# Keeping the recurrence layer in its emitted order on every engine, in a two-layer backbone kernel

## The chip, the cores and the metric

The kernel runs on one core of one Trainium2 chip. The metric is device time in microseconds (us) of one execution, and a comparison is made on medians of several runs on the same chip. The core has a matrix engine (TensorE, PE in the profile; its weight loads are shown apart as PEld), a vector engine (VectorE, DVE), a scalar engine (ScalarE, ACT), a further vector engine (GpSimd, POOL) and a queue that issues DMAs (SyncE, SP). Each engine takes its own instructions strictly in order, and waits on semaphores for what other engines and DMAs have to deliver.

## The reference, cut to what matters

Two layers over a context of 256 tokens and a latent sequence of 256 tokens, width 1024, each a mixer followed by a squared-ReLU MLP. Layer 0 mixes with a diagonal state space layer, layer 1 with a gated DeltaNet, which is the recurrence that the change is about. It has 8 key heads and 16 value heads of 128, chunks of 64 tokens, and both directions:

```python
q, k, v, z, gates = h @ w_in            # projections, a short centred conv on q, k, v, l2 norm of q, k
lower = strict(k_beta @ k.T * decay)    # one 64x64 triangle for each chunk and head
t_mat = triangular_solve(lower + eye, eye)
u, w = t_mat @ (v * beta), t_mat @ (k_beta * exp(g))
for each chunk:                          # the chain: one step after the other
    v_new = u_i - w_i @ state
    out_i = (q_i * exp(g)) @ state + attention(q_i, k_i) @ v_new
    state = state * exp(g_last) + k_end.T @ v_new
y = gated_rmsnorm(out, z) @ w_out
```

## The kernel before, in words

Layer 1's recurrence is `gdn_phase` (2003). It treats the 8 key heads with their two value heads each as 8 pairs p = 0 to 7. The weights stream from HBM: `w_load` (1086) loads one 128x1024 block on SP into one of four buffers `wraw`, and `w_split` (1096) makes it two parts in two buffers each, `whi` on ACT and `wlo` in two halves on POOL or DVE, after which `gdn_proj` (1566) multiplies it on PE, three products for each (`hh,whi`, `hl,whi`, `hh,wlo`). There are 49 such projections, 1200 matmuls: for each pair one of keys and two of values with 512 columns, one of queries and two of the output gate `z` with 256, and one for the decay gates. `post_qk`, `post_v`, `post_z` (1623, 1682, 1697) take them from PSUM: ACT copies to `pp`, DVE runs the five-tap conv as steps on `cacc`, and normed heads are transposed. `gdn_gates` (1463) makes the decays on DVE once at the start.

The triangular solve is `gdn_t` (1708), for each pair and each direction d. It loads decay rows by DMA on SP (tile `X`, from `grd`), makes `X` on POOL, DVE and ACT, `N` on DVE and POOL, `U` on DVE, its transpose `T`, and then squares up on PE with `A`, `T` and `U` going through DVE between the matmuls (`ap`, `up`, `wp`), down to `ub`. `X` and `N` have two buffers. The serial part is `gdn_chain` (1793), one for each value head, both heads of a pair side by side. Each of its eight laps multiplies the state with the keys (`c<-S,kt`), makes the residual `r` on DVE, multiplies by the solve's `ub` (`c<-r,ub`), scales to `v` on ACT, multiplies with the keys (`c<-v,kn`) and updates the state `S` on DVE. Three chains may be open at once. `gdn_read` (1867) makes the outputs and `gdn_out` (1909) the product with `w_out` at the end.

Two orders exist. The kernel's own planner, `drive` (316), runs these tasks as generators on a model of the clock, picks whose step can start first, ties going to the lower priority number, and emits the step's instructions. With `clock.fill` set (2096) the model may place a step in an earlier gap of its engine, so that the emitted order is not the order of its planned times. That stretch ends when all solves of pair 7 and all 49 projections have ended; what is left of the layer is emitted with `fill` off (2099). Behind the planner stands the tile scheduler of the compiler. It is given a priority with each instruction, `base + prio * 20000 + n` (263), where n counts the emitted instructions and `prio` is 0 for chains and weight loads, 1 for solves, 2 for reads, 3 for the steps after projections and the splits, 4 for projections and 5 for w_out. It moves instructions on an engine's queue by it. `follow` (124) ties a few PE instructions to earlier ones. The call by which every engine's instruction is emitted is `Engine.call` (259).

Of the kernel before, what the change touches and what calls it, by code (L numbers as in the profile page):

```python
# [252 lines left out]
class Engine:  # L253
# [3 lines left out]
    def __getattr__(self, op):  # L257
        f = getattr(self.eng, op)
        if not callable(f):
            return f  # L260

        def call(*args, **kw):
            c = self.clock
            p = c.issue(self.name, op, args, kw)
            if c.prio is not None:
                c.tc.cur_priority = c.base + c.prio * 20000 + c.n
                c.n += 1
            r = f(*args, **kw)  # L268
            if c.window is not None and self.name == "tensor" and c.prio is not None:
                c.follow(p[0], r.ins)  # L270
            return r
        return call
# [1944 lines left out]
```

## Time and profile before

| What | us |
|---|---|
| median of three runs | 1634.49 |
| the three runs | 1637.27, 1630.75, 1634.49 |
| the profiled execution | 1630.61 |
| its span in the trace | 1628.8 |
| PE busy in the span | 1467.9 |
| DVE busy | 1105.0 |
| ACT busy | 777.4 |
| POOL busy | 654.3 |

The span runs from the first to the last instruction in the trace, 1.8 us less than the execution's time. Layer 1's recurrence begins at about 752 us with its first projection; its first chain starts at about 898, its last projection ends near 1324, and the product with w_out ends near 1428. Before it lie layer 0 and the vectors of the modulation, behind it the last MLP. Busy shares over the whole span mix these stages, so a stretch is read with the busy time of that stretch.

### The profile page before, as it was taken

The page shows a single profiled execution, that of the slowest core. Times are in us where ns is not written, and L with a number is a line of the kernel's source. Part 1 is how long each engine was busy: PE and PEld are TensorE (multiplying, and loading weights), DVE is VectorE, ACT ScalarE, POOL GpSimd, SP SyncE. Part 2 cuts the span into 40 slices and gives each one's busy share as a digit, 9 for nine tenths or more (in the row PEclk, how much of TensorE's full clock was granted, in tenths as well). Part 3 has the DMA queues.
Part 4 walks back from the last instruction along what each step waited for, and adds up shares of the span by engine and source line. Part 5 has one row for each costly group of instructions (what it writes and reads, how often), then busy time and mean ns, then how long its engine had stood idle before and what let it go on. Part 6 is the DMA issues. An engine that isn't in the chain of part 4 may idle for free.

```text
span 1628.8 us, 31232 instructions
## 1 busy us (share of the span) xinstructions
PE 1467.9 (90%) x12370; PEld 1115.7 (68%) x12370; DVE 1105.0 (68%) x2011; ACT 777.4 (48%) x1637; POOL 654.3 (40%) x510
## 2 busy tenths in 40 slices
PE   6895678989999999997968898989999999989998
PEld 2454456767777777786756676767766665689997
DVE  6977798763343343347998878687869765667666
ACT  3352646543222232216456655656565755554443
POOL 3977033622333233334766543343615400014432
PEclk7997889999999999998989999999998999989999
DMA  9786623463544545331222211111211111536552
GB/s 279 264 290 91 137 98 118 156 211 113 172 147 170 188 158 181 139 106 65 79 77 67 66 54 47 53 47 50 70 39 59 44 57 61 188 127 196 182 192 91
DMA packets 76771, 200.77 MB, mean 123 GB/s; under 512 B 8784, under 2 KB 29008, under 8 KB 76368
## 3 DMA queue, kind: packets, MB, share of 16 engines
q1 hardware_dynamic: 76112, 197.78, 37.1%
q10 hardware_dynamic: 512, 0.98, 0.4%
q8 instruction: 97, 1.59, 0.4%
q14 instruction: 50, 0.41, 0.1%
HBM read 192.71 MB, written 6.03 MB: 122 GB/s over the span
## 4 chain that ended last, share of the span: by engine, by line
PE 62%; DVE 20%; ACT 6%; issue 5%; POOL 4%; DMA 3%; SPq 0%; POOLq 0%; DVEq 0%; ACTq 0%
PE w L268 32%; PE proj L268 8%; PE c L268 6%; DVE cacc L268 3%; PE ada L268 3%; DVE X L268 3%; PE wo L268 2%; POOL wlo L268 2%; DVE wlo L268 1%; DVE U L268 1%; DVE scanm L268 1%; DVE gt L268 1%; PE op L268 1%; PE qs L268 1%; DMA wraw<-in_w_dram 1%
## 5 line engine op out<-in xcount | busy, mean ns | idle before, releaser
L268 ACT CAST whi<-wraw 128x1024 fp32r<-128x1024 f32 x221 | 225.6, 1045 | 259.7 <-PE w L268 140.0
L268 POOL TENSOR_TENSOR wlo<-wraw,whi 128x512 fp32r<-128x512 f32 x129 | 181.7, 1427 | 258.4 <-ACT whi L268 233.6
L268 DVE TENSOR_TENSOR wlo<-wraw,whi 128x1024 fp32r<-128x1024 f32 (+1 forms) x189 | 222.0, 1202 | 79.9 <-ACT whi L268 79.3
L268 PE MATMUL w<-hh,whi 128*128 128x256 f32 (+1 forms) x512 | 170.5, 336 | 0.0
L268 PE MATMUL w<-hl,whi 128*128 128x256 f32 (+1 forms) x512 | 168.9, 331 | 0.0
L268 PE MATMUL w<-hh,wlo 128*128 128x256 f32 (+1 forms) x512 | 168.5, 331 | 0.0
L268 POOL TENSOR_TENSOR sq<-rl 128x512 f32<-128x512 f32 (+1 forms) x64 | 62.5, 977 | 217.1 <-ACT rl L268 213.3
L268 PE MATMUL w<-whi,h1h 128*128 128x512 f32 x384 | 148.8, 395 | 0.0
L268 PE MATMUL w<-whi,h1l 128*128 128x512 f32 x384 | 148.5, 390 | 0.0
L268 PE MATMUL w<-wlo,h1h 128*128 128x512 f32 x384 | 148.4, 389 | 0.0
L268 PE MATMUL proj<-hh,whi 128*128 128x256 f32 (+1 forms) x360 | 130.6, 363 | 10.3 <-ACT pp L268 8.4
L268 DVE TENSOR_TENSOR ma<-w,g 128x512 f32<-128x512 f32 x96 | 65.3, 687 | 103.5 <-PE w L268 103.4
L268 PE MATMUL proj<-hh,wlo 128*128 128x256 f32 (+1 forms) x360 | 125.5, 349 | 1.7 <-POOL wlo L268 1.7
L268 PE MATMUL proj<-hl,whi 128*128 128x256 f32 (+1 forms) x360 | 126.9, 352 | 0.0
L268 DVE SCALAR_TENSOR_TENSOR cacc<-pp,cw,cacc 128x520 f32<-128x520 f32 (+1 forms) x128 | 115.3, 903 | 11.5 <-ACT cacc L268 9.9
L268 POOL TENSOR_TENSOR xr<-xr,ma 128x512 f32<-128x512 f32 x56 | 81.3, 1455 | 95.9 <-DVE ma L268 95.9
L268 PEld LDWEIGHTS w<-hh,whi 128*128 128x128 f32 x512 | 98.0, 192 | 18.1 <-DVE wlo L268 4.2
L268 DVE TENSOR_TENSOR h1l<-sq,h1h 128x512 fp32r<-128x512 f32 (+1 forms) x64 | 35.5, 555 | 106.4 <-POOL sq L268 104.0
L268 PEld LDWEIGHTS w<-hl,whi 128*128 128x128 f32 x512 | 98.2, 192 | 10.5 <-issue 1.9
L268 PEld LDWEIGHTS w<-hh,wlo 128*128 128x128 f32 x512 | 97.9, 192 | 9.8 <-issue 0.8
L268 ACT ACTIVATE v<-c,vsc 64x128 f32<-64x128 f32 x224 | 80.6, 362 | 50.0 <-PE c L268 42.6
L268 POOL TENSOR_TENSOR rstd<-ms,mhalf 128x1 f32<-128x1 f32 (+2 forms) x22 | 17.3, 788 | 191.1 <-DVE ms L268 191.1
(312 smaller groups left out, 3532.2 us busy)
## 6 DMA issues: line engine op xcount, KB each, us to landing
wraw<-in_w_dram SPq DMA_DIRECT2D x128, 512.0 KB, 4.3
adaw<-in_ada_w_dram SPq DMA_DIRECT2D x92, 512.0 KB, 4.8
wraw<-in_w_in_dram SPq DMA_DIRECT2D x48, 512.0 KB, 3.2
wraw<-in_w_glu_dram SPq DMA_DIRECT2D x32, 512.0 KB, 3.3
wraw<-in_w_out_dram SPq DMA_DIRECT2D x16, 512.0 KB, 3.2
Kt<-kd SPq DMA_DIRECT2D x32, 128.0 KB, 4.9
X<-grd SPq DMA_DIRECT2D x32, 128.0 KB, 3.0
V<-in_ada_w_dram SPq DMA_DIRECT2D x4, 512.0 KB, 5.9
```

The lines of the kernel that those rows point to most:

```text
L268: r = f(*args, **kw)
```

## The change

While `clock.fill` is set and a task is running, each instruction is tied to the one that was emitted before it on the same engine. The tie carries no semaphore, since the engine takes its instructions in order; it only forbids the scheduler to put it ahead. The emission itself is the same in both kernels. No instruction, buffer or DMA is added or removed. The tie covers PE, DVE, ACT, POOL and SP, from the first step of `gdn_phase` up to the last projection and the last solve.

```diff
--- before.py
+++ after.py
@@ -266,6 +266,8 @@
                 c.tc.cur_priority = c.base + c.prio * 20000 + c.n
                 c.n += 1
             r = f(*args, **kw)
+            if c.fill and c.prio is not None:
+                c.tc.keep_in_program_order(r)
             if c.window is not None and self.name == "tensor" and c.prio is not None:
                 c.follow(p[0], r.ins)
             return r
```

The first place is SP's queue, from the DMAs that carry the decay rows (`grd<-gt`) on; `X<-grd x4` are the loads of a pair's two solves, `wraw` those of the projections' weights, `od<-yo` a DMA of the outputs.

```order
 L268 DMA grd<-gt 64x1x64 x4
-L268 DMA X<-grd 64x4x128 x4
 L268 DMA wraw<-in_w_in_dram 128x1024 x4
 L268 DMA X<-grd 64x4x128 x4
+L268 DMA wraw<-in_w_in_dram 128x1024 x7
+L268 DMA X<-grd 64x4x128 x4
+L268 DMA wraw<-in_w_in_dram 128x1024
+L268 DMA od<-yo 128x256 x2
+L268 DMA wraw<-in_w_in_dram 128x1024
+L268 DMA X<-grd 64x4x128 x2
+L268 DMA wraw<-in_w_in_dram 128x1024
+L268 DMA X<-grd 64x4x128 x2
```

Pair 0's X loads followed the decay rows at once and those of pair 1 four weight loads later; now pair 0's have four weight loads ahead of them and pair 1's eleven, and from pair 2 on the two directions' loads stand apart, each behind the weight load that was emitted ahead of it.

The second place is PE's queue in a middle lap of pair 0's chain. `c_6456` and `c_6457` are the two heads, and `ap` and `up` belong to the solves of later pairs. Before:

```order
L268 MATMUL ap<-T,nb_6452 128x64
L268 MATMUL c_6456<-r_8257,ub_8036 64x128
L268 MATMUL c_6456<-r_8257,ub_8055 64x128
L268 MATMUL proj<-hh,whi 128x512
...
L268 MATMUL proj<-hh,whi 128x512
L268 MATMUL c_6457<-S_8237,kt 64x128 x2
L268 LDWEIGHTS A
L268 MATMUL up<-U,A 64x64
L268 MATMUL c_6456<-v_6460,kn 128x256
```

After, where `kTp` is a transpose of the next pair's keys:

```order
L268 MATMUL kTp<-consts,kn 128x2x64 x4
L268 MATMUL c_6456<-S_8233,kt 64x128 x2
L268 MATMUL c_6457<-S_8237,kt 64x128 x2
L268 MATMUL c_6456<-r_8257,ub_8036 64x128
L268 MATMUL c_6456<-r_8257,ub_8055 64x128
L268 MATMUL c_6457<-r_8264,ub_8036 64x128
L268 MATMUL c_6457<-r_8264,ub_8055 64x128
L268 MATMUL c_6456<-v_6460,kn 128x256
L268 MATMUL c_6457<-v_6462,kn 128x256
L268 MATMUL kTp<-consts,qn 128x2x64 x2
```

The products of both heads, which had projections and solves between them, now follow each other, from one S to the next. From the first to the last matmul of pair 0's chain there were 810 matmuls on PE, and there are 354.

The third place is POOL's queue at the start of the layer, where `hl<-hf,hh` and `rstd` belong to the norm ahead of it and `wlo` are the splits of the first weight blocks.

```order
 L268 TENSOR_TENSOR hl<-hf,hh 128x4x128
 L268 TENSOR_TENSOR rstd<-ms,mhalf 128x1
-L268 TENSOR_TENSOR wlo<-wraw,whi 128x512 x2
+L268 TENSOR_TENSOR hl<-hf,hh 128x4x128
 L268 TENSOR_TENSOR rstd<-ms,mhalf 128x1
-L268 TENSOR_TENSOR hl<-hf,hh 128x4x128 x3
+L268 TENSOR_TENSOR hl<-hf,hh 128x4x128 x2
 L268 MEMSET pp_6440 128x524
 L268 MEMSET pp_6442 128x524
```

The two splits that stood among the norm's operations now stand behind it and behind the initial values of buffers and constants that begin with the last rows shown.

## Rows read from the trace of the kernel before

**Rows 1.** The page, busy us, share of the span, instructions.
```profile
PE 1467.9 (90%) x12370; PEld 1115.7 (68%) x12370; DVE 1105.0 (68%) x2011; ACT 777.4 (48%) x1637; POOL 654.3 (40%) x510
```

**Rows 2.** Busy us by stretch: PE, PEld, DVE, ACT, POOL, PEclk, DMA, GB/s.
```profile
752.00:809.00 57.00, 51.01 (x303) 44.83 (x302) 52.02 (x73) 28.43 (x64) 34.57 (x39) 0.95 0.26 85
809.00:984.00 175.00, 149.78 (x1548) 115.63 (x1546) 148.09 (x252) 103.18 (x245) 97.27 (x73) 0.92 0.19 64
984.00:1324.00 340.00, 319.01 (x3947) 231.75 (x3946) 267.42 (x593) 214.51 (x572) 136.10 (x106) 0.97 0.15 49
1324.00:1428.00 104.00, 96.11 (x684) 63.13 (x682) 60.35 (x152) 53.33 (x129) 4.89 (x5) 0.98 0.37 123
```

**Rows 3.** PE's waits, 752 to 1430 us: total, times, longest.
```profile
PE ap L268 <- DVE T L268: 12.0, 8, 2.9
PE proj L268 <- ACT pp L268: 8.4, 6, 5.1
...
PE c L268 <- DVE r L268: 5.8, 4, 3.9
PE c L268 <- ACT v L268: 4.2, 12, 0.7
```

**Rows 4.** Timeline, DVE and POOL, 740 to 790: start, length.
```profile
740.40 1.69 POOL L268 TENSOR_TENSOR wlo<-wraw,whi 128x512 fp32r<-128x512 f32 x1 [2.46 <-ACT whi L268]
...
759.19 0.44 POOL L268 TENSOR_SCALAR id1k<-c 128x64 f32<-128x64 f32 x1
...
788.00 5.11 DVE L268 SCALAR_TENSOR_TENSOR cacc<-pp,cw,cacc 128x520 f32<-128x520 f32 x4
```

**Rows 5.** Timeline, pair 0's X loads and first transpose.
```profile
799.97 2.68 SPq L268 DMA_DIRECT2D X<-grd  x4
...
838.40 0.70 DVE L268 STREAM_TRANSPOSE T<-U 128x512 f16<-128x512 f16 x1
```

**Rows 6.** The chain that ended last, in time, 740 to 1430.
```profile
1093.38 4.30 PE proj L268 x18
...
1318.50 2.23 PE proj L268 x18
```

**Rows 7.** Timeline, PE, 1277 to 1279.
```profile
1277.19 0.44 PE L268 MATMUL c<-S,kt 128*64 128x128 f32 x4
...
1277.93 0.43 PE L268 MATMUL wp<-U,E 64*64 64x64 f16 x15
1278.30 0.70 PE L268 MATMUL c<-v,kn 128*128 128x256 f32 x2
```

**Rows 8.** Groups by shape, 752 to 1430: busy us, mean ns, idle.
```profile
L268 POOL TENSOR_TENSOR wlo<-wraw,whi 128x512 fp32r<-128x512 f32 x95 | 131.7, 1407 | 164.6 <-ACT whi L268 144.4 <-PE c L268 8.0 <-PE ep L268 4.7
L268 DVE SCALAR_TENSOR_TENSOR cacc<-pp,cw,cacc 128x520 f32<-128x520 f32 x96 | 95.9, 1000 | 7.8 <-ACT cacc L268 6.7
...
L268 ACT CAST whi<-wraw 128x1024 fp32r<-128x1024 f32 x63 | 65.7, 1043 | 28.6 <-PE proj L268 18.2 <-issue 4.7 <-POOL lo L268 2.7
...
L268 DVE TENSOR_TENSOR U<-N,c 128x512 f16<-128x512 f32 x16 | 17.1, 1068 | 1.9 <-PE up L268 1.0 <-POOL N L268 0.9
...
L268 ACT ACTIVATE X<-X 128x512 f32<-128x512 f32 x16 | 10.0, 631 | 13.8 <-DVE X L268 13.7
```

**Rows 9.** Tile c, 752 to 1430: ns min/median/max, first, last.
```profile
L268 ACT ACTIVATE v<-c,vsc x224: 345/362/369, 910.8 to 1385.6; 64x128 f32<-64x128 f32 x112
...
L268 DVE SCALAR_TENSOR_TENSOR S<-S,egl,c x192: 299/341/349, 925.1 to 1388.2; 128x128 f32<-128x128 f32 x192
L268 DVE SCALAR_TENSOR_TENSOR r<-c,neg,vs x112: 304/344/354, 921.6 to 1391.6; 128x128 f32<-128x128 f32 x112
...
L268 PE MATMUL c<-vs,ub x64: 269/269/320, 898.3 to 1343.4; 64*64 64x128 f32 x64
...
L268 POOL TENSOR_TENSOR X<-X,c x16: 1255/1600/2677, 804.0 to 1241.6; 128x512 f32<-128x512 f32 x16
```

**Rows 10.** Tile cacc, the same columns, whole run.
```profile
L268 DVE SCALAR_TENSOR_TENSOR cacc<-pp,cw,cacc x128: 443/754/1897, 758.9 to 1248.8; 128x520 f32<-128x520 f32 x96, 128x262 f32<-128x262 f32 x32
```

## The prediction, made before the changed kernel ran

> **What bounds the kernel now.** First the page, for the engine that carries the span: TensorE (PE) is busy 90% of it [rows 1]. Then busy time by stage, which says where that average misleads [rows 2]. The change acts between 752 and 1428 us. From 752 to 984 VectorE (DVE) binds as much as PE: it is busy 52.0 of 57 and 148.1 of 175 us, PE 51.0 and 149.8, and PE's clock is granted at 0.92 in the longer piece. From 984 to 1324 PE binds, with 319.0 of 340 us. The tail to 1428 is PE again, 96.1 of 104. What the change could win is therefore small and can be written down: PE idles 6 + 25 + 21 + 8 = 60 us there. The waits tell what ends that idle time: DVE operations of the solve (T), a projection buffer that ACT still reads (pp), and chain operations (r, v) [rows 3]. No single wait is large. The order that the scheduler makes interleaves everything, so a late operand rarely has nothing beside it.
>
> **The change part by part.** No instruction is added or removed. Each one that is emitted before the last projection now stands behind the one emitted before it on its engine. Four terms follow from the orders of both kernels, priced by rows of this trace. Counts of matmuls are the order's; a float32 one of a chain shows as two records in the trace (c<-S,kt x4 for two).
>
> *Start of the layer.* Two things cost. First, the splits of the first weight blocks ran on POOL at 740.40, in gaps of the norm; they now stand behind the last norm operations and the constants, which end at 759.63 [rows 4]. The first projection, which began at 752, then waits for its wlo, some 5 us, since its products with whi can go ahead. Second, the X loads of pair 0 now stand behind four more weight loads on SP, the last of which waits for a buffer that projection 9 frees indirectly; so X, issued at 799.97 now [rows 5], comes some 10 us later. Both are partly covered, since the gates' DVE chain has only one conv step in it where it had four (5.1 us, [rows 4]). I take +10 together. Against that, DVE needs fewer rows to reach the first chains: from pair 0's X to its last ub there are 140 rows before and 80 now, since the convs of pairs 2 and 3 and the first steps of pairs 1 and 2 are put off; from there to the first r of pair 1 115 and 117. This DVE-bound stretch, 809 to 984, took 175 us for its 252 instructions, 0.69 us each [rows 2]; 58 rows fewer are 40 us. But they are put off, not dropped: ahead of pair 1's chain PE has done 504 projection matmuls instead of 648. The 144, half of 512 columns at 4.30/18 = 0.24 us and half of 256 columns at 2.23/18 = 0.12 us [rows 6], are 26 us that PE must still do when it binds. Sum: 10 - 40 + 26 = -4, bounds -25 (start costs hidden) and +15 (DVE rows not the limit).
>
> *Feed of the solves.* Before, SP issues X up to two pairs ahead; between the projection whose end frees the buffer and the first matmul of a solve stand 584 to 1336 matmuls. Now each X load is put just behind a weight load. That load waits for the split four blocks earlier, which waits for the end of a projection six back (four wraw, two whi buffers). From there to the solve's first matmul 92 to 285 matmuls are left. For pair 3 they are 24 and 12 projection matmuls of 0.24 and 0.12 us, 30 chain ones of 0.22 and 4 of 0.70, 121 of other solves at 0.03 and 26 others at about 0.1 [rows 6, 7]: 23 us; the seven pairs lie between 20 and 31. The path beside it is whi 1.04, two wlo 2.81, the landing of X 2.7, POOL X and N 1.60 each (N taken as X), three DVE steps (X, N, U, all taken as U's 1.07), ACT X 0.63 and the first T 0.70 [rows 5, 8, 9]: 14.3 us if no queue holds it. That leaves 6 to 17 us for ten hops through four queues. How much do queues take? Pair 0 went from X issued at 799.97 to its first T at 838.40, 38 us for what alone takes 10.4 [rows 5], though it was not urgent then. Four of the first solves have their POOL X right behind the very wlo that frees the load, so POOL idles a landing, 2.7 us. For pairs 2 to 7 I take 2 us each, +12; bounds 0 (the slack holds) and +36 (6 us each, a path of 29 us against 23).
>
> *Laps of the chains.* A lap, from S to the next S, is 0.44 (S,kt) + 0.34 (r) + 0.44 (r,ub) + 0.72 (two v) + 0.70 (v,kn) + 0.68 (two S) = 3.3 us without hops; the matmul groups are taken as rows 7 show S,kt and v,kn, with r,ub, as many records, like S,kt, and the rest is from [rows 9]. Before, pair 0's chain spread over 810 matmuls, 192 of them projections, and chains of neighbouring pairs overlap (45 to 83 foreign chain matmuls in each of pairs 1 to 6). Now it spans 354, with 24 projections, and no foreign chain. In its middle laps both heads' four matmul groups follow each other with at most a few transposes between: 4 x 0.44 + 2 x 0.70 = 3.2 us of work at most, against 3.3 of lap and its hops [rows 7]. I take 0.75 us idle in each of its eight laps, 6 us. Pairs 1 to 6 have 96 to 120 projections and a solve inside, enough on average, not in every lap: 1 us each, 6 more. So +12; the low bound is -10, half of the 21 us that PE idles from 984 to 1324 [rows 2], should the new order hide waits better; the high one +35, 5 us a pair from operations that wait on DVE behind conv steps of 1.0 us mean [rows 8].
>
> *Tail.* After the last matmul of the solves 104 chain and read matmuls and 192 of w_out remain in the new order; in the old one there are 106 and 192 and, besides, 43 of pair 6's chain that serve as cover for pair 7's laps. 43 x 0.22 us are 9 us; half of it is lost, I take +4, bounds -5 (the cover was not needed, and the work is out of the tail) and +12.
>
> Sum: -4 + 12 + 12 + 4 = +24 on the profiled 1630.6, 1654.6. That execution lies 3.9 under the median of 1634.5, so **1658**.
>
> At one place the Trainium skill speaks for another price. The conv step cacc takes 443 to 1897 ns, 754 in the median, while S and r stay within 299 to 354 [rows 9, 10]. The page "SBUF — State Buffer", section "Who interferes with whom", says that a DVE instruction with two SBUF inputs and a GpSimd one that reads SBUF shut each other out, and that issue order decides who waits. The spread of cacc agrees. By that rule a new order of POOL beside DVE alone can shorten the convs, by up to 12 us; by the sum above it leaves them as they are, at nothing. What it gives is a rival below.
>
> **The rivals.** *Faster: the idle goes.* The emitted order comes from a plan with a clock of its own; if laps and feeds fit, PE idles less. For: PE and DVE are both busy but not full, and pair 0's chain moves forward by 40 us. Against: the slack counted above. Price: start -20, laps -10, the rest nothing: 1634.5 - 30 = 1604, or half of it, 1619. It decides if the solves' path stays under 20 us.
> *No change.* Laps and feeds cost what the start gains, within 8 us of 1634.5: 1634. For: the work on each engine is the same, and PE binds for most of the stage.
> *Lock-step: much slower.* In-order queues wait for one another in a ring: a late projection delays the weight load, the X behind it on SP, the solve, the chain, and with it the next projections, all behind one another on PE. Price: feed +36 and laps +35 with the rest unchanged, 1634.5 - 4 + 71 + 4 = 1706. It decides from a path of 28 us on.
> *Convs shortened by POOL's new order.* If the 96 long cacc fell from 1.00 us in the mean to the median 0.754 [rows 8, 10], DVE saves 24 us, half of it in the DVE-bound start: 1658 - 12 = 1646.
>
> **How the numbers follow.** Forecast, slower by 9 to 45 us: 0.42. Convs shortened: 0.06. Lock-step: 0.14. No change: 0.16. Faster: 0.22. Runs of this kernel tell about 0.5%, 8 us, from no change; so faster 0.22, same 0.16, slower 0.42 + 0.06 + 0.14 = 0.62. The range should leave out 0.2: it reaches from 1616, which takes in half of the faster case, to 1708, just past the lock-step; the likeliest case alone spans 1643 to 1680.
>
> **What would show it.** Start: POOL's first wlo of the layer after the constants, the first projection held by wlo, the first chain matmul before 880 instead of at 898.3 [rows 9]. Feed: PE waits for DVE T well above 12.0 in 752 to 1430 [rows 3], and POOL X waiting for its DMA. Laps: more PE waits for r and v than the present 5.8 and 4.2 [rows 3], and pair 0's chain done within 60 us. The last projection matmul, now just before 1324, where the third window ends [rows 2], should come later by about as much as the whole is slower, less the tail. I am wrong if PE's busy share from the first chain to the last projection rises: then the plan's order is the better one and the time falls below 1626. I am also wrong if the loss sits in the tail, or in DVE at unchanged PE waits.

## The result

The changed kernel takes 1833.64 us in the median (1828.88 to 1836.71), the kernel before, with a fourth run beside the three shown, 1632.74. The ratio is 1.1205, with a 95% interval of 1.1165 to 1.1244 (the two medians alone give 1.123): 12% slower. The prediction said slower, by 1.4%, and its range ended at 1708.

The page of the changed kernel, the rows that answer to [rows 1] (busy us, share of the span, instructions), with DVE's beside it:

```profile
PE 1527.5 (84%) x12370; PEld 1140.8 (62%) x12370; DVE 1076.4 (59%) x2011; ACT 784.5 (43%) x1637; POOL 638.9 (35%) x510
```

The work is the same and the span 198 us longer. DVE is busy 29 us less than before. PE is busy 60 us longer for the same 12370 instructions, at a lower granted clock, below. The stages show where the span grew. Busy us by stretch (PE, PEld, DVE, ACT, POOL, then PEclk, the granted clock of PE, DMA share, GB/s) of the kernel before, cut at its first chain and its last projection; the tail that follows is the last line of [rows 2]:

```profile
751.00:898.00 147.00, 120.32 (x941) 101.05 (x939) 134.01 (x193) 81.46 (x186) 93.31 (x81) 0.89 0.22 73
898.00:1324.00 426.00, 400.49 (x4857) 292.16 (x4858) 333.74 (x725) 265.41 (x697) 175.32 (x136) 0.97 0.16 52
```

and of the changed kernel, cut at the same events:

```profile
751.00:927.00 176.00, 128.15 (x945) 104.20 (x945) 112.89 (x175) 73.23 (x165) 73.06 (x66) 0.81 0.17 58
927.00:1524.00 597.00, 460.21 (x5026) 323.29 (x5025) 338.24 (x772) 285.26 (x735) 181.06 (x150) 0.88 0.12 40
1524.00:1626.00 102.00, 88.57 (x511) 56.91 (x507) 51.05 (x119) 45.36 (x104) 4.90 (x5) 0.90 0.37 126
```

From the first projection to the first chain it is 147 us before and 176 now; from the first chain to the last projection 426 and 597; the tail 104 and 102. So 171 of the 198 us lie in the middle. There DVE's busy time hardly moves (334 and 338 us), and its idle time goes from 92 to 259 us. PE's idle time goes from 26 to 137 us, and its busy time from 400 to 460; 169 of its instructions (x5026 against x4857) have come into this stage, nearly all from the tail (x684 and x511), whose busy time falls by 7.5 us.

The waits of PE in the changed kernel from 751 to 1626 us, answering to [rows 3] (total, times, longest):

```profile
PE proj L268 <- ACT pp L268: 51.5, 21, 9.8
PE proj L268 <- DVE zs L268: 26.9, 13, 4.4
PE ap L268 <- DVE T L268: 21.0, 19, 2.3
PE c L268 <- ACT v L268: 11.9, 10, 5.0
PE c L268 <- DVE r L268: 10.7, 14, 4.1
```

The three waits that the prediction priced, T, r and v, were 12.0, 5.8 and 4.2 us and are 21.0, 10.7 and 11.9: up by 22 us in all. The largest is another: a projection waits for its one PSUM buffer, which an ACT or DVE operation of the step after the last projection has not yet read, 78 us in all against 8.4 for pp and 1.6 for zs before. DVE's own waits in the middle stage, before:

```profile
DVE S L268 <- PE c L268: 22.6, 30, 2.5
DVE r L268 <- PE c L268: 21.4, 20, 4.1
DVE A L268 <- PE ap L268: 2.4, 7, 0.6
```

and after:

```profile
DVE r L268 <- PE c L268: 48.0, 28, 5.0
DVE S L268 <- PE c L268: 44.6, 41, 4.2
DVE A L268 <- PE ap L268: 25.5, 29, 4.8
DVE zs L268 <- ACT zth L268: 18.7, 11, 3.9
DVE yo L268 <- DMA od<-yo: 16.2, 6, 6.6
```

Waits for PE's chain products double (22.6 and 21.4 to 44.6 and 48.0 us), and the one for the solves' product ap goes from 2.4 to 25.5. New among the largest are zs waiting for ACT's half of the same step, 18.7 us, and the output yo waiting for the DMA of the yo before it, 16.2 us.

One such place shows how a wait travels. DVE in the changed kernel, 1375 to 1386 (start, length, and in brackets the idle time ahead and what ended it):

```profile
1376.85 0.48 DVE L268 SCALAR_TENSOR_TENSOR yo<-ot,on,zs 128x256 f32<-128x256 f32 x1 [1.02 <-PE ot L268]
1383.89 0.48 DVE L268 SCALAR_TENSOR_TENSOR yo<-ot,on,zs 128x256 f32<-128x256 f32 x1 [6.56 <-DMA od<-yo]
1384.29 0.34 DVE L268 SCALAR_TENSOR_TENSOR r<-c,neg,vs 128x128 f32<-128x128 f32 x1
1384.55 1.55 DVE L268 SCALAR_TENSOR_TENSOR cacc<-pp,cw,cacc 128x520 f32<-128x520 f32 x2
```

The second yo has one buffer with the first, and can start only when the first has gone out. SP's queue there:

```profile
1379.95 0.33 SPq L268 DMA_DIRECT2D wraw<-in_w_in_dram  x1
1380.38 0.38 SPq L268 DMA_DIRECT2D od<-yo  x1
```

and POOL's:

```profile
1377.44 2.48 POOL L268 TENSOR_TENSOR wlo<-wraw,whi 128x512 fp32r<-128x512 f32 x2 [2.32 <-ACT whi L268]
```

The DMA of yo stands behind a weight load. That load is issued at 1379.95, just after POOL has ended the split that gives a weight buffer back, at 1379.92. DVE is idle for 6.56 us. Behind yo in its queue stand the chain's r and two conv steps. PE and ACT at the same place:

```profile
1386.13 0.64 ACT L268 ACTIVATE cth<-cacc 128x520 f32<-128x520 f32 x1 [7.75 <-DVE cacc L268]
1386.67 0.35 ACT L268 COPY pp<-proj 128x256 f32<-128x256 f32 x1
```

```profile
1377.68 0.69 PE L268 MATMUL c<-S,kt 128*64 128x128 f32 x4 [0.31 <-ACT S L268]
1387.08 0.80 PE L268 MATMUL proj<-hh,whi 128*128 128x512 f32 x1 [8.70 <-ACT pp L268]
...
1390.49 0.44 PE L268 MATMUL c<-r,ub 64*64 64x128 f32 x4
```

The product c<-S,kt that r needs was done at 1378.37; r started at 1384.29. ACT had nothing but the conv's last step in front, and waited 7.75 us for it, with the copy pp of the next projection result behind it. PE waited 8.70 us for that copy, with a projection in front, and r's product c<-r,ub, which could have run at 1384.63, stood behind the projection until 1390.49. A weight buffer that came free late has stopped SP, DVE, ACT and PE in turn. This is one place of many: with SP's queue left to the scheduler most of the loss is still there (e4, below). The page "PSUM — Partial Sum Buffer" of the Trainium skill, section "Engine vs sequencer instructions", calls the queues of ScalarE, VectorE and GpSimdE strict FIFO; the place agrees, with r 5.9 us behind its operand.

The clock follows. Pair 0's chain in the changed kernel, windows of 10 us (the columns as above):

```profile
935.00:945.00 10.00, 6.14 (x33) 4.05 (x31) 3.96 (x10) 3.91 (x15) 3.54 (x3) 0.91 0.11 29
945.00:955.00 10.00, 7.04 (x34) 4.06 (x34) 4.32 (x15) 6.95 (x18) 4.42 (x4) 0.50 0.16 52
...
965.00:975.00 10.00, 9.29 (x158) 6.81 (x160) 8.04 (x20) 4.59 (x12) 0.00 (x0) 0.89 0.01 2
```

PE is busy 6.1 and 7.0 of 10 us, and the granted clock goes from 0.91 to 0.50, the lower of its two levels (1.2 GHz against 2.4), and it is 0.89 where PE is busy 9.3 of 10. In the whole middle stage it is 0.88 and was 0.97.

### The profile page after: what moved, and what is told of

Same layout as the page of the kernel before. It is cut to its first block, busy times and chain, and to the rows that moved or that the text cites. A ratio compares the mean times of both kernels' runs of the same rounds, so it can differ in the third digit from the quotient of the medians.

```text
span 1827.1 us, 31192 instructions
## 1 busy us (share of the span) xinstructions
PE 1527.5 (84%) x12370; PEld 1140.8 (62%) x12370; DVE 1076.4 (59%) x2011; ACT 784.5 (43%) x1637; POOL 638.9 (35%) x510
## 5 line engine op out<-in xcount | busy, mean ns | idle before, releaser
L268 POOL TENSOR_TENSOR wlo<-wraw,whi 128x512 fp32r<-128x512 f32 x129 | 177.6, 1395 | 376.2 <-ACT whi L268 335.6
L268 PE MATMUL proj<-hh,whi 128*128 128x256 f32 (+1 forms) x360 | 152.5, 424 | 83.1 <-ACT pp L268 51.5
L268 PEld LDWEIGHTS proj<-hh,whi 128*128 128x128 f32 x360 | 78.5, 218 | 111.1 <-ACT pp L268 57.5
L268 PE MATMUL proj<-hh,wlo 128*128 128x256 f32 (+1 forms) x360 | 133.5, 371 | 3.0 <-POOL wlo L268 3.0
L268 PE MATMUL proj<-hl,whi 128*128 128x256 f32 (+1 forms) x360 | 134.2, 373 | 0.0
L268 DVE SCALAR_TENSOR_TENSOR cacc<-pp,cw,cacc 128x520 f32<-128x520 f32 (+1 forms) x128 | 108.7, 853 | 9.3 <-ACT cacc L268 7.8
```

## The experiments

In the table the kernel before of the same job is subtracted (1632.7 us for the change; 1637.8, 1637.4, 1640.3, 1635.5 and 1635.0 in the five jobs of the experiments). Most kernels ran twice, the change four times, e6 five and i2 eight times. No interval holds 1.

| kernel | us | ratio to before, 95% | over before |
|---|---|---|---|
| the change | 1833.6 | 1.1205 (1.1165 to 1.1244) | +201 |
| e1, PE only | 1712.6 | 1.0459 (1.0403 to 1.0516) | +75 |
| e2, all but PE | 1837.1 | 1.1220 (1.1159 to 1.1280) | +199 |
| e3, SP only | 1662.4 | 1.0153 (1.0091 to 1.0215) | +25 |
| e4, all but SP | 1827.3 | 1.1160 (1.1084 to 1.1237) | +190 |
| e7, DVE only | 1816.1 | 1.1116 (1.1059 to 1.1174) | +179 |
| e8, POOL only | 1657.6 | 1.0146 (1.0089 to 1.0204) | +20 |
| e9, ACT only | 1755.6 | 1.0709 (1.0659 to 1.0759) | +115 |
| e5, all, heads of solves free | 1852.2 | 1.1338 (1.1279 to 1.1397) | +215 |
| e6, 14 ties on heads alone | 1645.4 | 1.0049 (1.0016 to 1.0082) | +8 |
| g1, DVE in planned order | 1785.2 | 1.0890 (1.0831 to 1.0948) | +145 |
| g3, DVE, chains, solves, reads | 1720.4 | 1.0495 (1.0410 to 1.0579) | +80 |
| g4, DVE, each kind for itself | 1707.8 | 1.0418 (1.0366 to 1.0470) | +68 |
| i1, DVE, solves | 1670.4 | 1.0200 (1.0134 to 1.0267) | +35 |
| i2, DVE, chains and gates | 1647.2 | 1.0065 (1.0036 to 1.0094) | +12 |
| h1, other plan costs, all tied | 1804.4 | 1.1019 (1.0949 to 1.1089) | +169 |
| h2, other plan costs, no tie | 1654.3 | 1.0102 (1.0039 to 1.0166) | +19 |
| j, DVE, 8 places back | 1710.7 | 1.0460 (1.0423 to 1.0497) | +76 |
| j, DVE, 32 places back | 1654.4 | 1.0116 (1.0067 to 1.0164) | +19 |

### Which engine's order

Four kernels tie a part of the engines. The edit is the condition (`tensor` is PE, `vector` DVE, `scalar` ACT, `gpsimd` POOL, `sync` SP):

```diff
-            if c.fill and c.prio is not None:
+            if c.fill and c.prio is not None and self.name == "tensor":   # e1
+            if c.fill and c.prio is not None and self.name != "tensor":   # e2
+            if c.fill and c.prio is not None and self.name == "sync":     # e3
+            if c.fill and c.prio is not None and self.name != "sync":     # e4
                 c.tc.keep_in_program_order(r)
```

PE only:

> Only PE's instructions are tied, the four other engines stay with the scheduler. Theory A, PE in emitted order stands behind projections whose one PSUM buffer is not yet read (63 us of such waits after, 8 before): most of the 200 us, 1760 to 1840. Theory B, the X loads late on SP make the solves late: under 1660, since SP is free. Theory C, the queues hold one another, no engine alone is enough: 1650 to 1730.

All but PE:

> DVE, ACT, POOL and SP are tied, PE is left to the scheduler. Theory A: little, 1630 to 1680. Theory B: nearly all, 1760 to 1840. Theory C: in between, 1680 to 1780.

SP only:

> Only SP's DMAs are tied. Theory A and C: 1630 to 1650. Theory B: 1720 or more, with solves that begin one after the other as in the changed kernel.

All but SP:

> PE, DVE, ACT and POOL are tied, SP is left to the scheduler. Theory A: 1810 to 1840. Theory B: below 1700. Theory C: 1760 to 1830.

PE's order alone costs 75 us; the other four engines' without PE's cost the whole 199. Theory A, by which PE stands at the projections' buffer, falls: the 78 us of such waits are where the loss shows on PE, and with PE free the loss is as large, though PE's waits for pp are 5.5 us there. SP's order costs 25 us alone, more than the 12 of the prediction's feed, but the whole without it still costs 190 of 201. Theory B falls too, though e2 came out in its range. Theory C, that no engine is enough, has its range in e1 and e4 and misses it in e2 and in e3, where all three miss; it was left, with the four other engines together open.

### The heads of the solves

On DVE, the X of pair 2's first solve stands ahead of pair 1's last steps (E) in the kernel before; in the changed one the X of a solve stands behind the last steps of the solve of the pair before, of its direction. That made theory D: the ties put the head of a solve (X, N and U, some 20 us) behind the end of the solve before it. Two kernels test it from both sides, and two more go on with single engines. `behind` ties an instruction to the last one of the same key, with the same NoSync edge; `head` is set at the start of `gdn_t` and cleared ahead of its first T. In these kernels the line of `Engine.call` has the number 274.

```diff
-            if c.fill and c.prio is not None:
-                c.tc.keep_in_program_order(r)
+            if c.fill and c.prio is not None and not getattr(c.task, "head", False):   # e5
+                c.behind(self.name, r.ins)
+            if c.fill and c.prio == 1 and self.name == "vector":                       # e6
+                if c.task is not c.tied.get(("task", c.task.d)):
+                    c.tied["task", c.task.d] = c.task
+                    c.behind(c.task.d, r.ins)
+                c.tied[c.task.d] = r.ins.name
```

All tied but the heads:

> As the changed kernel, but the head of every solve (its X loads on SP and all its operations on POOL, DVE and ACT ahead of the first T) is not tied and nothing is tied to it. Theory D, the ties put the head of a solve behind the end of the solve before it, where the scheduler ran it beside that solve, and so add some 20 us to each of seven pairs: 1690 to 1750, 80 to 140 less than the changed kernel. Theory C, the queues hold one another everywhere, so that freeing a few instructions helps little: above 1790.

Only the heads tied, by 14 ties:

> As the kernel before, with 14 ties only: the first DVE operation of a solve (X) behind the last DVE operation of the solve of the pair before, of the same direction. Theory D: 1710 to 1790, most of what the head costs, with nothing else tied. Theory C: within 20 us of the kernel before.

DVE only:

> Only DVE's instructions are tied. Theory D: its queue alone holds the heads behind the solves before, 1740 to 1840. Theory C: no engine alone is enough, 1650 to 1730 as PE alone.

POOL only:

> Only POOL's instructions are tied. POOL's last operation of a solve (ibd) stands ahead of the five rounds, so by theory D its order need not hold a head behind the end of the solve before: 1640 to 1700. Theory C: as any other engine, 1650 to 1730; if POOL's order of weight splits is what delays, above 1740.

Neither run gives theory D its number. With free heads the kernel is slower still, 1852 us, and they did run ahead; POOL's X of the solves in the changed kernel and in e5 (ns min/median/max, first and last start):

```profile
L268 POOL TENSOR_TENSOR X<-X,c x16: 1256/1267/1712, 849.6 to 1468.2; 128x512 f32<-128x512 f32 x16
```

```profile
L274 POOL TENSOR_TENSOR X<-X,c x16: 1252/1270/1625, 810.6 to 1331.0; 128x512 f32<-128x512 f32 x16
```

The last one starts at 1331.0 instead of 1468.2, and it does not help. The 14 ties alone cost 8 us. So the operations of the heads are not what costs.

That does not clear the distance between solves, for e5 did not close it. From the end of ub, the last DVE operation of a solve, to the first T of the next pair's solve of the same direction, the traces show 28 and 2 us before (two directions, each the sum of seven steps), 165 and 219 in the changed kernel, 154 and 209 with DVE alone tied (e7, below), and 158 and 212 in e5, with the heads long done. In e6 it is 66 and 61. The rounds themselves, from the first T to ub, take no longer: 470 and 493 us in all before, 469 and 452 after. One such step on DVE, from pair 1 to pair 2, before:

```profile
971.54 0.68 DVE L268 SCALAR_TENSOR_TENSOR ub<-wp,U 128x512 f32<-128x512 f32 x1
972.14 0.70 DVE L268 STREAM_TRANSPOSE T<-U 128x512 f16<-128x512 f16 x1
```

and after:

```profile
1008.18 0.69 DVE L268 SCALAR_TENSOR_TENSOR ub<-wp,U 128x512 f32<-128x512 f32 x1 [1.60 <-PE wp L268]
...
1023.22 0.68 DVE L268 TENSOR_TENSOR U<-N,c 128x512 f16<-128x512 f32 x1
1027.78 0.42 DVE L268 SCALAR_TENSOR_TENSOR zs<-zth,proj 128x256 f32<-128x256 f32 x1 [3.89 <-ACT zth L268]
1031.86 1.18 DVE L268 SCALAR_TENSOR_TENSOR S<-S,egl,c 128x128 f32<-128x128 f32 x4 [3.65 <-PE c L268]
...
1033.27 0.70 DVE L268 STREAM_TRANSPOSE T<-U 128x512 f16<-128x512 f16 x1
```

The U that T needs is made by 1023.90; T starts 9.4 us later, behind a zs that waits for ACT and laps of pair 1's chain that wait for PE. In the order of the kernel before, the first T's of the fourteen later solves pass 2 to 50 DVE instructions that were emitted ahead of them, most of them of the chains. The distance alone does not set the price: g3 below has 143 and 220 us of it and costs 80, e1 has 13 us and none and costs 75.

DVE only is the finding: 1816 us, a loss of 179 us alone, against 201 with all five tied. POOL's order costs 20, which both theories allow. Theory D had the right number for DVE only; by the two runs before, its reason, the heads' own operations, does not hold, though solves that begin late do show. DVE only, from its first chain to its last projection:

```profile
930.30:1503.90 573.60, 470.74 (x4913) 331.48 (x4913) 333.59 (x760) 282.13 (x726) 175.07 (x146) 0.85 0.12 39
```

DVE is busy 334 us as before and idle 240, PE busy at a granted clock of 0.85. PE's waits there:

```profile
PE c L268 <- DVE r L268: 13.1, 14, 5.2
PE c L268 <- ACT v L268: 11.7, 17, 1.6
PE c L268 <- DVE S L268: 9.5, 8, 3.4
PE up L268 <- DVE A L268: 7.9, 15, 0.9
PE c L268 <- ACT vn L268: 7.6, 17, 0.9
```

With PE free, the waits for the projection buffer are not among its largest; those are for r, v, S, A and vn, 50 of PE's 103 us of idle time. The queue that causes the loss and the wait in which it shows are on different engines.

### Which order, and which kinds

```diff
-            if c.fill and c.prio is not None:
-                c.tc.keep_in_program_order(r)
+            if c.fill and c.prio is not None and self.name == "vector":       # g1
+                c.plan.setdefault(self.name, []).append((p[0], c.n, r.ins))   # tied in a row by p[0] after the stage
+            if c.fill and c.prio in (0, 1, 2) and self.name == "vector":      # g3
+                c.behind(self.name, r.ins)
+            if c.fill and c.prio is not None and self.name == "vector":       # g4
+                c.behind(c.prio, r.ins)
+            if c.fill and c.prio is not None and self.name == "scalar":       # e9
+                c.tc.keep_in_program_order(r)
```

DVE in the order of the planned start times:

> Only DVE's instructions are tied, but in the order of the start times that the planner gave them, not in the order in which it emitted them (only DVE in emitted order: 1816). Theory E, the emitted order is not the planned one, and what was planned into an earlier gap stands too late on DVE: well below 1750. Theory F, any one fixed order on DVE loses, since operations come in at other times than the plan has them: 1780 or more.

DVE's chains, solves and reads:

> Only DVE's operations of chains, solves, reads and gates are tied to one another in emitted order; its convs and the other steps after projections are free. Theory F1, two latency-bound rows of operations, chain laps and solve rounds, are locked one to one: 1760 to 1820. Theory F2, urgent operations stand behind the convs of 1 us and their waits: under 1690.

DVE, each kind for itself:

> Only DVE's operations are tied, each to the one emitted before it of its own kind (chains and gates among themselves, solves, reads, steps after projections): each kind keeps its order, the kinds pass one another freely. Both F1 and F2, the loss lies between kinds: under 1680. If it lies within a kind (two solves or three chains locked to one another): above 1740.

ACT only:

> Only ACT's instructions are tied. If ACT's order locks the kinds as DVE's does, 1740 to 1820; if DVE is the special one because it is busy 79 percent between the first chain and the last projection and ACT 63: 1650 to 1720.

The planned order in place of the emitted one takes 1785 us, where theory F has 1780 or more. It brings back 34 of 179 us, so theory E holds for a fifth of the loss. Theory F, that any one fixed order loses, isn't shown by it: the planned order is close to the emitted one (169 of 954 instructions run ahead of one emitted earlier, and none passes more than 16), and the scheduler's order in the kernel before is fixed before the run as well. Chains, solves and reads tied to one another cost 80 us with the convs free, so neither F1 (1760 and more) nor F2 (under 1690) has it alone. Ties within each kind cost 68, which neither expected. ACT's order costs 115 us, in the range of an order that locks as DVE's does: DVE is not the only engine that can hold the stage. The single costs (75, 25, 179, 20, 115) sum to twice the whole, so they aren't shares. The scheduler places the other queues around the one that is tied, and DVE's order gives way with it: 401 DVE instructions pass eight or more others before, 120 with PE alone tied and 53 with ACT alone tied.

Two more take the kinds apart, and two ask whether the order is bad because the planner's clock is. The clock's edit:

```diff
-    LAT, LATF = 0.12, 0.182
+    LAT, LATF = 0.12, 0.09
...
                     cost = (66 - 4 * psum + n * (6 if op == "reciprocal" else 0.5 if flat and not psum else 1)) / 960
...
+                    cost += 0.09
                 elif eng == "scalar":
-                    cost = (0.051 if psum else 0.093) + 0.093 * extra + n / 1200
+                    cost = (0.051 if psum else 0.093) + 0.093 * extra + n / 1200 + 0.1
```

With it and all ties:

> As the changed kernel, all engines tied, but the planner's clock gives each DVE and ACT operation the 0.09 and 0.10 us that the trace shows it to take more, and a hop between engines as much less. Theory G, the emitted order locks because the plan's DVE and ACT are too light (the plan packs them fuller than they can run): 1690 to 1770. Theory H, the order locks however well its clock fits: 1800 or more.

With it and no tie:

> The same clock without any tie, so the scheduler orders the new emission: what the emission alone does. Both theories: 1620 to 1660, as the kernel before, since the scheduler makes its own order.

DVE's solves alone, and DVE's chains and gates alone (`c.prio == 1` and `c.prio == 0` in the condition, with `behind`):

> Only DVE's operations of the solves are tied, to one another. If the two directions' solves, whose rounds then take turns, make up the 67 us that ties within kinds cost: 1680 to 1710. If it is chains or convs: within 15 us of the kernel before.

> Only DVE's operations of the chains and gates are tied, to one another. If laps of the heads and neighbouring pairs, which then take turns, make up the 67 us: 1680 to 1710. If it is solves or convs: within 15 us of the kernel before.

The ties cost 201 us with the old costs, and 1804 - 1654 = 150 with the new ones. So the planner's clock may have a part, about a quarter, and theory H stands for the rest: at 1804 us it is not a matter of 0.1 us an operation. Within the kinds the solves make 35 us, half of what was asked of them, and chains with gates 12, which by the expectation rules them out; the convs and reads, not run alone, would be left with some 20 of the 68 if the parts add.

### How far an instruction must be able to move

By the order of the kernel before, 702 of DVE's 954 instructions of the stage run ahead of one emitted before them, 401 ahead of eight or more, 232 ahead of 32 or more; it is the solves and the convs that go far (they pass 30 and 52 others in the mean), while chain operations pass two. The last two kernels tie each DVE instruction not to the one before it but to the one 8 or 32 places back:

```diff
-            if c.fill and c.prio is not None:
-                c.tc.keep_in_program_order(r)
+            if c.fill and c.prio is not None and self.name == "vector":
+                c.back(8, r.ins)      # 32 in the other: tied to the instruction emitted so many places before
```

> Only DVE is tied, and each of its instructions not to the one emitted before it but to the one eight places back, so that it may pass seven. In the kernel before, 702 of DVE's 954 instructions of the stage run ahead of something emitted earlier, 401 of them ahead of eight or more. Theory K, what is lost is turn taking, small swaps when an operand comes a little late: 1640 to 1670. Theory M, what is lost is reach, work of later steps brought far ahead to fill a wait: 1720 or more.

> The same with 32 places (232 of the 954 pass 32 or more in the kernel before). Theory K: as the kernel before, 1630 to 1650. Theory M: still 1670 or more.

Neither theory has it alone. One place costs 179 us, eight 76, 32 places 19. Other than the expectation says, these ties do not bound how far an instruction moves: every eighth instruction keeps its order, which makes eight strands, and strands may pass one another. In the order of the kernel with eight places 567 of the 954 run ahead of one emitted earlier, 51 pass eight or more, and the most that one passes is 20; with 32 places it is 642, 327 pass eight or more, 31 pass 32 or more, and the most is 54 (192 before). So 103 of the 179 us come back with reach that is mostly under eight (theory K), another 57 with reach mostly under 32 (theory M), and the last 19 need more still. DVE's largest waits, with eight places:

```profile
DVE S L274 <- PE c L274: 51.6, 42, 4.8
DVE r L274 <- PE c L274: 35.2, 26, 4.6
DVE A L274 <- PE ap L274: 13.8, 14, 4.8
```

and with 32:

```profile
DVE S L274 <- PE c L274: 37.0, 31, 5.2
DVE r L274 <- PE c L274: 26.9, 19, 5.6
DVE A L274 <- PE ap L274: 10.9, 13, 3.1
```

and with one place, the kernel of DVE only (927 to 1524 us, 20 us beyond its stage, where the middle line is 45.6):

```profile
DVE S L268 <- PE c L268: 51.9, 34, 6.5
DVE A L268 <- PE ap L268: 48.9, 28, 6.5
DVE r L268 <- PE c L268: 27.7, 13, 5.8
```

The wait for the solves' product ap, ahead of A, falls from 48.9 to 13.8 us with eight places and 10.9 with 32. That for the chains' products ahead of S stays at 51.6 with eight and falls to 37.0 with 32, and the one ahead of r is 35.2 and 26.9 against 27.7. By these waits the short moves let the solves' rounds through, and the longer ones part of the chains' laps; no run separates the two.

## Why the prediction was wrong, point by point

**The sign and the mechanism.** Slower was right, and the rival called lock-step, given 0.14 and 1706 us, described the ring that the timeline above shows: a late buffer delays a weight load, what stands behind it on SP, the solve or the chain, and the projections. But the link through SP is not what costs, since 190 of the 201 us stay without it (e4). The step that failed is the pricing of the middle stage, feed and laps, +24 together where +171 was measured: a fixed order was priced by what PE would wait for, and DVE's queue, whose order alone costs 179 us (e7), was left out of the sum there.

**The omission.** The terms price waits of PE, with a hop's delay for each queue passed. DVE's own order has a term only at the start of the layer, where it was a gain; in the middle stage it stands in the high bound of the laps alone, as 5 us a pair behind conv steps, 35 in all. But DVE was busy 334 of 426 us in the middle stage, and its idle time there was 92 us and became 259 for the same work: the scheduler's order had given it a ready operation where the emitted one makes it wait. By e7 the loss of that alone is 179 us, with PE, ACT, POOL and SP free. The prediction said that no single wait is large because everything is interleaved [rows 3], and then priced the change by those same small waits. They did grow, as its signs have it, but T, r and v by 22 us in all.

**Start, -4 with bounds -25 and +15.** The first chain starts 176 us after the first projection instead of 147: +29. The POOL row was right (the first wlo stands behind the constants, and PE was held 3.05 us for it, 5 were forecast), but the credit of 40 us for 58 DVE rows fewer was not: DVE's busy time up to the first chain fell from 134.0 to 112.9 us, and its idle time rose from 13 to 63. A queue of fewer rows isn't sooner through if each row waits. The first chain was to come before 880 and came at 927.3.

**Feed, +12 with bounds 0 and +36.** SP's order alone costs 25 us (e3), inside the bounds, and without it 190 of 201 us are left (e4). What the term took to be 2 us a pair, a first T that comes late, came as 24 and 31 us a step in the two directions (165 and 219 over seven, 4 and none before). The term followed the head from its load to T; T's own place on DVE, behind chain laps and convs, had no price, and e5 shows that a head done early does not help.

**Laps, +12 with bounds -10 and +35.** This term, taken together with the feed, was to be the middle stage: +24, and it is +171, of which 111 are PE's idle time and 60 its busy time, in part work from the tail, for the rest the lower clock. The laps themselves did not grow. Pair 0's chain was done within 60 us, as said, and from DVE's first S to its last the chains of the eight pairs take 432 us in all before and 422 after. From the last S of a pair to the first of the next it is 31 us over the seven steps before and 223 after. The time went in between the chains and not into their laps. The clock had no term at all, although its rows show it at 0.92 where PE was busy 150 of 175 us and at 0.97 where it was busy 319 of 340 [rows 2].

**Tail, +4.** It is -2, inside the bounds.

**The convs.** The 96 long cacc went from 1000 to 936 ns in the mean [rows 8]:

```profile
L268 DVE SCALAR_TENSOR_TENSOR cacc<-pp,cw,cacc 128x520 f32<-128x520 f32 x96 | 89.6, 936 | 8.8 <-ACT cacc L268 7.8
```

That is 6 us, in the direction of the rule of the Trainium skill's page "SBUF — State Buffer", section "Who interferes with whom", with POOL less dense beside DVE (181 of 597 us of the middle stage, 175 of 426 before). No run here separates the rule from other reasons.

**What stays open.** Shown is that DVE's order alone is enough for most of the loss, that ACT's and PE's alone cost 115 and 75 us, and that looser ties on DVE buy the loss back in steps. Not shown is a single pair of operations that locks; the loss lies within the kinds (68 us) and between them. The late first T of each solve goes with the loss, but no run freed it alone. Nor was a kernel run with all engines tied but DVE, so that DVE's order may be enough without being needed. Whether the lower clock adds to the loss or only comes with it was not tried.

## What to carry to other kernels

Both kernels run each queue in an order that was fixed before the run; what the change gave up is the scheduler's choice of it. An operand that comes late stops all that stands behind it in its queue, and then other engines. Before keeping an emitted order, look at every engine and not only the one that carries the span, and ask what fills its waits now: if instructions pass tens of others there, that reach is what is given up, and the small waits of the present profile say little about its price. DVE, busy 78% of the middle stage here, and ACT, busy 62%, each cost more alone than PE. The engine whose waits grow need not be the one that causes them: PE's waits for one buffer grew by 68 us here, and with PE free the kernel was as slow.

## What the runs showed of the hardware

In this kernel one queue in the emitted order was enough to slow the stage: DVE's alone cost 179 us and all together 201. PE's granted clock over the middle stage was 0.97 before, with 26 us of idle time in 426, 0.88 in the changed kernel, with 137 in 597, and 0.85 with DVE alone tied, with 103 in 574; in the changed kernel the same 12370 instructions took 60 us more busy time, at waits for a buffer of no more than 10 us each. No version that was run beat the kernel before.
